# A branch product's operand pages in another order, its weight parts cut earlier, and the first down weights requested a unit ahead

## The chip, the core and the metric

The kernel runs on one core of one Trainium2 chip. Such a core has a matrix engine (TensorE, PE in the profile, with its weight loads as PEld), three engines for elementwise work (VectorE = DVE, ScalarE = ACT, GpSimd = POOL), a queue engine that only issues transfers (SyncE = SP) and 16 DMA engines that all transfers share. SBUF is the on-chip memory of 128 partitions; PSUM, in banks, takes what TensorE computes. Each engine takes its instructions in the order in which the program lists them. The metric is the time of one execution in device microseconds; lower is better.

## The reference

One layer of a streaming encoder on 1024 prompt rows and 32 sample rows (1056 columns in the kernel), float32. Cut to what surrounds the change:

```python
h = _rms_norm(x, g_pre_mix)
z = h @ w_in                       # q_A k_A v_A q_B f_B i_B og_B gate_A gate_B
ya = _sink_attention(...)          # branch A, 16 heads, window of 3 chunks
yb = _hgrn2(...)                   # branch B, gated linear recurrence
mix = jax.nn.sigmoid(ga) * (ya @ w_br_a) + jax.nn.sigmoid(gb) * (yb @ w_br_b)
x = x + _rms_norm(mix @ w_out, g_post_mix)
a, u = jnp.split(_rms_norm(x, g_pre_ffn) @ w_up, 2, axis=-1)
ac = b_conv + sum(ap[:, j:j + t] * w_conv[j] for j in range(3))
x = x + _rms_norm((jax.nn.gelu(ac) * u) @ w_down, g_post_ffn)
x = x + (pe @ w_ple) * jax.nn.sigmoid(x @ w_ple_gate)
```

## The kernel before

All products run at float32 precision on TensorE out of two parts: each operand is cut into a high part (a cast on ScalarE) and a low part (the operand less its high part, a subtraction on VectorE), and three matmuls (high x high, high x low, low x high) make one product. The large products are done in Strassen's manner: seven products of half-size blocks in place of eight, from sums of blocks that are made beforehand and kept in DRAM.

The program goes through these stages: the input product with attention and recurrence woven in; the last gate blocks (`stream(tail...)`, matmuls L205 to L207, results X, Y, Z evacuated by ScalarE into `gt` at L297 and stored to `tb_d`); the branch product `ya @ w_br_a` (`a_unit`, matmuls L1616 to L1620); `yb @ w_br_b`, the output product, the up product with 22 units (`up_unit`, L2297 to L2299), the down product (`d_unit`, L2418 to L2420) and the last gate.

**Operands of the branch product.** `opa[i, p]` is the operand of product i (0 to 6) for half p of the columns: a page `oa` of 128 x 2 x 4 x 264 floats. `a_load` (L1528) takes the page and asks for a transfer of 528 KB into its second half; `a_split` (L1537) casts the high part into the first half (L1534, ScalarE) and subtracts (L1535, VectorE). Pages have names such as r6 or l0; the r-pages lie in a pool `rp` on the right side of SBUF, where the tiles of the stages before lay. A page gets its address when its name is first asked for, in the order of asking; a transfer into it waits until the old tiles at that address have been read or stored for the last time. Before, the names were asked for as the loads were: r6, r1, r3, r5, r7 for the first five (issued on GpSimd), then r4, r0, r2 on SyncE.

**Weight parts.** `a_raw` (L1504) loads a pair of raw blocks `wa` (2 x 256 KB, two buffers, SyncE), `a_prepare(n)` (L1514) casts and subtracts the next block into `wt` (L1522, L1523), and asks for a further pair ahead. Eight buffers hold `wt`.

**What sets the order.** The dictionary `small` hangs work on the pieces of the last three gate blocks; `during` does the same for the steps of the branch product. `behind(S, V)` ties work to the last instruction of ScalarE and VectorE. Between these ties, a scheduling layer places every instruction in its engine's order, transfers too, so the order of the code isn't the order on an engine. In the branch product the bank of a first result is freed by a copy `as` (L1625, ScalarE).

**Down weights.** `d_raw` (L2050) loads a pair of raw blocks `wd`; before, the first call came out of `d_prepare` from step 4 of the last up unit on.

Of the kernel before, what the change touches and what calls it, by code (L numbers as in the profile page):

```python
# [17 lines left out]
P = 128  # L18
# [12 lines left out]
H = 264  # L31
# [28 lines left out]
def layer_kernel(  # L60
# [256 lines left out]
    with right("ap") as ap:  # L317
# [279 lines left out]
        def pinned(f, *engines):  # L597
            with behind(*engines):
                f()
# [333 lines left out]
        blocks, small = [(lambda w=w: w, 2, out) for w, out in zip(ws, outs)], {}  # L933
# [138 lines left out]
    small = {2 * n: [lambda n=n: pinned(lambda: b_prepare(n), V)] for n in range(3)}  # L1072
# [14 lines left out]
    with right("bp") as bp:  # L1087
# [309 lines left out]
        pieces, small = [], {}  # L1397
# [82 lines left out]
    def page(pool, n, shape, name):  # L1480

        s = f"{'r' if pool is rp else 'l'}{n}"
        s = home.get(s, s)
        return (rp if s[0] == "r" else lq).tile(shape, F32R, tag=f"pg{s[1:]}", name=nm(name))

    def page_at(s, shape, name):
        return page(rp if s[0] == "r" else lq, s[1:], shape, name)

    def columns8(s, name):
# [9 lines left out]
    at_a = {0: ("r6", "r5"), 1: ("r1", "r7"), 2: ("r3", "r4"), 3: ("r0", "r2"), 4: ("l0", "l1"),  # L1499
            5: ("l2", "l3"), 6: ("l4", "l5")}  # L1500
# [24 lines left out]

    opa = {}

    def a_load(i, p, queue=dma):  # L1528
        t = opa[i, p] = page_at(at_a[i][p], [P, 2, 4, H], "oa")
        src = sa_d[i][:, :, p] if i in sa_d else ya_v[:, min(i, 1), i // 6][:, :, p]  # L1530
        queue(t[:, 1].bitcast(F32), src)

# [7 lines left out]
    def both(f, *a):  # L1540
        with behind(S, V):
            f(*a)

    small = {}
    first_a = [(i, p) for p in range(2) for i in range(3)]
    for i, p in first_a[:5]:
        a_load(i, p, gdma)
    for m, (i, p) in enumerate(first_a[:5]):
        small[m + 1] = [lambda i=i, p=p: both(a_split, i, p)]
    for m in range(3):  # L1550
        small[m + 1].append(lambda m=m: both(a_prepare, m))
    for m, (i, p) in enumerate(((2, 1), (3, 0), (3, 1))):
        small[m + 3].append(lambda i=i, p=p: a_load(i, p))
    stream(tail[3:], small)
    lctx.close()
    pctx.close()
# [3 lines left out]
    with right("mp") as mp:  # L1560
# [91 lines left out]
        def during(s, f, *a):  # L1652
            steps_a.setdefault(s, []).append((f, a))
# [13 lines left out]
            both(load_next)  # L1667

        for n, (i, p) in enumerate((i, p) for i in (4, 5, 6) for p in range(2)):
            during(2 * n, a_load, i, p)  # L1670
            during(9 + n + n // 2, both, a_split, i, p)
        for n, (i, p) in enumerate(((2, 1), (3, 0), (3, 1))):
            during(2 * n + 1, both, a_split, i, p)
        for n in range(4):
# [375 lines left out]
    def d_raw():  # L2050

        k = len(raw_d)
        t = wp.tile([P, KT, P], F32, tag="wr", name=nm("wd"), bufs=2)
        raw_d.append(t)
        for a in range(2):
            pt, c, i = D_ORDER[2 * k + a]
            j0, n = KP[pt]
            z_ = slice(j0, j0 + n)
            src = w_d[i][:, c, z_] if i in w_d else dv[:, i // 2 % 2 + i // 5, i // 5, c, z_]
            dma(t[:, 4 * a:4 * a + n], src)  # L2060
# [52 lines left out]
    t = tr_bank()  # L2113
# [166 lines left out]
    def up_unit(u):  # L2280
        X, Y, Z = (pf.tile([P, 2, 512], F32, tag="st", name=nm("st"), bufs=3) for _ in range(3))
        ab = fp.tile([P, 4 + T], F32, tag="ab", name=nm("ab"), bufs=2)
        G.memset(ab[:, 0:2], 0.0)
        us = us0 if u == 0 else Up[:, u % 2, :].bitcast(F32)
        us4 = us.rearrange("p (a h c) -> p a h c", a=2, h=2)
        w = {}

        def mults(i, t, first, ps):
            n = 7 * u + i
            if i not in w:  # L2290
                w[i] = ready_w[n]
            for p in ps:
                for k in range(4):
                    wh, wl = w[i][:, 0, k, :], w[i][:, 1, k, :]
                    xh, xl = ops[p][i][:, 0, k, :], ops[p][i][:, 1, k, :]
                    o = t[:, p, 0:H]
                    E.matmul(o, wh, xh, start=first and k == 0, stop=False, skip_group_check=True)  # L2297
                    E.matmul(o, wh, xl, start=False, stop=False, skip_group_check=True)  # L2298
                    E.matmul(o, wl, xh, start=False, stop=k == 3, skip_group_check=True)  # L2299

        def v(t, ps):
            return t[:, ps[0]:ps[-1] + 1, 0:H]

        def after(i, ps):
            x, y, zz = v(X, ps), v(Y, ps), v(Z, ps)
            sl = slice(ps[0], ps[-1] + 1)
            if i == 0:
                S.copy(s1c[:, sl], x)  # L2308
            elif i == 1:
                V.tensor_tensor(U2[:, sl], s1c[:, sl], y, op=ALU.subtract)  # L2310
            elif i == 2:
                V.tensor_tensor(ab[:, 2:2 + T].rearrange("p (a h c) -> p a h c", a=2, h=2)[:, sl, 0, :],
                                x, rb4[:, sl, 0, :], op=ALU.mult)
            elif i == 3:
                V.tensor_tensor(nU3[:, sl], y, s1c[:, sl], op=ALU.subtract)
            elif i == 4:
                V.tensor_tensor(us4[:, sl, 1, :], nU3[:, sl], zz, op=ALU.subtract)
            elif i == 5:
                V.tensor_tensor(us4[:, sl, 0, :], y, s1c[:, sl], op=ALU.subtract)
            elif i == 7:  # L2320

                S.copy(t12[:, sl], zz)
            elif i == 8:
                V.tensor_tensor(nU3[:, sl], nU3[:, sl], t12[:, sl], op=ALU.add)
            else:
                V.tensor_tensor(t12[:, sl], U2[:, sl], zz, op=ALU.add)

        def done():

            V.tensor_tensor(ab[:, 2:2 + T].rearrange("p (a h c) -> p a h c", a=2, h=2)[:, :, 1, 0:232],  # L2330
                            t12[:, :, 0:232], rb4[:, :, 1, 0:232], op=ALU.mult)
            for p, o in ((0, 2 + 496), (1, 2 + 1026)):
                V.tensor_tensor(ab[:, o:o + 32], t12[:, p, 232:H], rb4[:, p, 1, 232:H], op=ALU.mult)
            tail_of.append(ff_tail(u, ab, us))
            next(tail_of[0])


        order = ((0, X, True, (0,)), (1, Y, True, (1,)), (2, X, False, (2,)), (3, Y, False, (3,)),
                 (4, Z, True, (4,)), (5, Y, False, (5,)), (6, Z, False, (6,)))
        first_ = order[:2] + ((2, X, False, ()),) + order[3:6] + ((6, Z, False, (2, 6)),)  # L2340
        early = ((0, X, True, (0,)), (6, Z, True, (7,)), (2, X, False, ()), (1, Y, True, (1,)),
                 (3, Y, False, (3, 8)), (4, Z, False, (4, 6)), (5, Y, False, (2, 5)))
        for ps, steps in (((0,), first_), ((1,), early)) if u == 0 else (((0, 1), order),):
            for n, (i, t, first, then) in enumerate(steps):
                if u:
                    prepare(7 * u + n + AHEAD)
                elif ps == (1,):
                    with behind(S, V):
                        prepare(n + AHEAD + 2)
                mults(i, t, first, ps)  # L2350
                if u == NF - 1:
                    if i < 3:
                        for p in range(2):
                            load_op(0, p, i)
                    if n in (3, 5, 6):
                        split_ops(0, {3: 0, 5: 1, 6: 2}[n])
                if ps == (1,) and n == 1:
                    with behind(E):
                        x1_t.append(pair_norm(1, 1.0 / D, late=True))
                if ps == (1,) and n == 4:  # L2360
                    with behind(E):
                        x1_t[0]()
                for a in then:
                    with behind(*((V,) if ps == (0,) and a == 2 else ())):
                        after(a, ps)
                if n == 1:
                    with behind(V):
                        tail_rest(u)
                if u == 1 and n == 3:
                    with behind(V):  # L2370
                        tail_rest(0)
                if u > 1 and n == 2 + u % 2:
                    if u % 2 == 0:
                        sums_of.append(act_sums(u // 2 - 1))
                    with behind(V):
                        next(sums_of[-1])
                if u == 0 and ps == (0,):
                    last_ops(n)
                if 2 <= u < 18 and n == 4:
                    w_sum((u - 2) // 2, 2 + u % 2)  # L2380
        done()
# [409 lines left out]
    t = tr_bank()  # L2791
# [26 lines left out]
    t = tr_bank()  # L2818
# [5 lines left out]
    t = tr_bank()  # L2824
# [40 lines left out]
```

## Time and profile before

| | |
|---|---|
| Time, median of 3 runs | 1954.24 us (1953.73 to 1957.8) |
| The profiled execution | 1954.29 us, its span 1952.5 us |
| TensorE busy | 1929.3 us |
| VectorE, ScalarE, GpSimd busy | 1452.2, 1012.4, 308.5 us |
| TensorE's longest wait | 5.0 us, at the first matmul of the branch product |
| DMA, mean | 155 GB/s, 302.19 MB |
| TensorE clock granted, mean | 0.998 of full |

The profile is of one execution. A view of waits names an engine and line, what it waited for, and microseconds in total, times, and the longest. In the timeline a row is: start, length, engine, line, operation, out<-in, shape, count, and in brackets the idle time ahead of it with what ended it. SPq is SyncE's queue of transfers; the time of such a row is that of the issue, not of the transfer.

### The profile page before, as it was taken

The page shows a single profiled execution, that of the slowest core. Times are in us where ns is not written, and L with a number is a line of the kernel's source. Part 1 is how long each engine was busy: PE and PEld are TensorE (multiplying, and loading weights), DVE is VectorE, ACT ScalarE, POOL GpSimd, SP SyncE. Part 2 cuts the span into 40 slices and gives each one's busy share as a digit, 9 for nine tenths or more (in the row PEclk, how much of TensorE's full clock was granted, in tenths as well). Part 3 has the DMA queues.
Part 4 walks back from the last instruction along what each step waited for, and adds up shares of the span by engine and source line. Part 5 has one row for each costly group of instructions (what it writes and reads, how often), then busy time and mean ns, then how long its engine had stood idle before and what let it go on. Part 6 is the DMA issues. An engine that isn't in the chain of part 4 may idle for free.

```text
span 1952.5 us, 38068 instructions
## 1 busy us (share of the span) xinstructions
PE 1929.3 (99%) x14619; PEld 1911.8 (98%) x14619; DVE 1452.2 (74%) x3160; ACT 1012.4 (52%) x2182; POOL 308.5 (16%) x419
## 2 busy tenths in 40 slices
PE   8999999999999999989999999999999999999998
PEld 8999999999999999989999999999999999999998
DVE  6777777788888888657655778778777786768872
ACT  7667777666656666543324763333333346534432
POOL 2111111010101110010001023343443410000000
PEclk9999999999999999999999999999999999999999
DMA  8534543433637563487749582434665357755343
GB/s 267 153 112 122 135 124 96 139 104 102 155 114 166 97 121 76 123 268 237 219 140 303 175 297 92 139 120 153 139 135 160 103 166 243 217 185 156 116 131 88
DMA packets 310507, 302.19 MB, mean 155 GB/s; under 512 B 14293, under 2 KB 276344, under 8 KB 310325
## 3 DMA queue, kind: packets, MB, share of 16 engines
q1 hardware_dynamic: 277269, 229.57, 37.8%
q0 software_dynamic: 32928, 70.14, 15.7%
q8 instruction: 115, 1.88, 0.4%
q14 instruction: 67, 0.55, 0.1%
q10 hardware_dynamic: 128, 0.06, 0.0%
HBM read 213.48 MB, written 115.16 MB: 168 GB/s over the span
## 4 chain that ended last, share of the span: by engine, by line
PE 86%; DVE 5%; DMA 3%; ACT 3%; issue 2%; POOL 0%; SPq 0%; ACTq 0%; DVEq 0%; POOLq 0%
PE st L2299 7%; PE st L2298 7%; PE st L2297 7%; PE mm L205 6%; PE mm L206 6%; PE mm L207 6%; PE st L2418 4%; PE st L2420 4%; PE st L2419 4%; PE Y L1119 2%; PE G L1122 2%; PE st L205 2%; PE G L1121 2%; PE Y L1122 2%; PE Y L1121 2%; PE G L1119 2%
## 5 line engine op out<-in xcount | busy, mean ns | idle before, releaser
L2297 PE MATMUL st<-op,wt 128*128 128x264 f32 x1232 | 348.9, 283 | 2.3 <-ACT Sp L2308 1.4
L2299 PE MATMUL st<-op,wt 128*128 128x264 f32 x1232 | 349.7, 284 | 0.0
L2298 PE MATMUL st<-op,wt 128*128 128x264 f32 x1232 | 347.6, 282 | 0.0
L2297 PEld LDWEIGHTS st<-op,wt 128*128 128x128 f32 x1232 | 231.2, 188 | 4.0 <-ACT Sp L2308 2.0
L2298 PEld LDWEIGHTS st<-op,wt 128*128 128x128 f32 x1232 | 231.4, 188 | 0.0
L2299 PEld LDWEIGHTS st<-op,wt 128*128 128x128 f32 x1232 | 230.8, 187 | 0.0
L2418 PE MATMUL st<-dop,wt 128*128 128x264 f32 x616 | 174.4, 283 | 1.2 <-ACT S L2433 1.2
L2420 PE MATMUL st<-dop,wt 128*128 128x264 f32 x616 | 174.3, 283 | 0.0
L2419 PE MATMUL st<-dop,wt 128*128 128x264 f32 x616 | 173.9, 282 | 0.0
L1965 ACT CAST wt<-wu 128x512 fp32r<-128x512 f32 x126 | 75.9, 618 | 178.1 <-POOL wu L1974 71.6
L205 PE MATMUL mm<-La,wh 128*128 128x384 f32 (+1 forms) x480 | 158.2, 330 | 0.0
L206 PE MATMUL mm<-Lb,wh 128*128 128x384 f32 (+1 forms) x480 | 155.3, 324 | 0.6 <-DVE Lb L781 0.6
L207 PE MATMUL mm<-La,wl 128*128 128x384 f32 (+1 forms) x480 | 154.9, 323 | 0.1
L1966 DVE TENSOR_TENSOR wt<-wu,wt 128x512 fp32r<-128x512 f32 x126 | 86.5, 695 | 46.7 <-ACT wt L1965 46.7
L2418 PEld LDWEIGHTS st<-dop,wt 128*128 128x128 f32 x616 | 115.6, 188 | 1.7 <-ACT S L2433 1.4
L2419 PEld LDWEIGHTS st<-dop,wt 128*128 128x128 f32 x616 | 115.7, 188 | 0.0
L2420 PEld LDWEIGHTS st<-dop,wt 128*128 128x128 f32 x616 | 115.4, 188 | 0.0
L2071 ACT CAST wt<-wd 128x512 fp32r<-128x512 f32 (+1 forms) x84 | 49.1, 586 | 90.6 <-PE st L2420 77.9
L206 PEld LDWEIGHTS mm<-Lb,wh 128*128 128x128 f32 x480 | 90.4, 189 | 1.7 <-DVE Lb L781 1.5
L207 PEld LDWEIGHTS mm<-La,wl 128*128 128x128 f32 x480 | 90.2, 188 | 0.5 <-DVE wl L756 0.5
L1119 PE MATMUL G<-La,wt 128*128 128x288 f32 x288 | 90.4, 314 | 0.0
L205 PEld LDWEIGHTS mm<-La,wh 128*128 128x128 f32 x480 | 90.2, 188 | 0.2
(602 smaller groups left out, 6249.9 us busy)
## 6 DMA issues: line engine op xcount, KB each, us to landing
wu<-in_w_up_dram SPq DMA_DIRECT2D x42, 512.0 KB
wu<-in_w_in_dram SPq DMA_DIRECT2D x36, 512.0 KB
w_d<-in_w_down_dram POOLq DMA_DIRECT2D x24, 704.0 KB, 6.8
a_d<-Up SPq DMA_DIRECT2D x22, 528.0 KB
wr<-in_w_in_dram SPq DMA_DIRECT2D x21, 512.0 KB
s_d<-sm SPq DMA_DIRECT2D x40, 264.0 KB
dop<-s_d SPq DMA_DIRECT2D x16, 528.0 KB
wr<-in_w_out_dram SPq DMA_DIRECT2D x16, 512.0 KB
```

Source lines behind the costliest of these rows:

```text
L205: E.matmul(ps, wh, a, start=first and n == 0, stop=False)
L206: E.matmul(ps, wh, b, start=False, stop=False)
L207: E.matmul(ps, wl, a, start=False, stop=last and n == len(ks) - 1)
L1119: E.matmul(o, wh, x[0][k], start=first and k == 0, stop=False, skip_group_check=True)
L1121: E.matmul(o, wh, x[1][k], start=False, stop=False, skip_group_check=True)
L1966: V.tensor_tensor(t[:, 1], src, t[:, 0].bitcast(F32), op=ALU.subtract)
L2297: E.matmul(o, wh, xh, start=first and k == 0, stop=False, skip_group_check=True)
L2298: E.matmul(o, wh, xl, start=False, stop=False, skip_group_check=True)
L2299: E.matmul(o, wl, xh, start=False, stop=k == 3, skip_group_check=True)
L2418: E.matmul(o, wh, xh_, start=first and k == 0, stop=False, skip_group_check=True)
L2419: E.matmul(o, wh, xl_, start=False, stop=False, skip_group_check=True)
L2420: E.matmul(o, wl, xh_, start=False, stop=k == ng - 1, skip_group_check=True)
```

## The change

`a_load` no longer takes the page; a new `a_page` does. The pages of the first three products and of product 3 are taken ahead of any load, in the order (3,0), (3,1), (2,1), (1,1), (0,1), (2,0), (1,0), (0,0), so that r0, r2, r4, r7, r5, r3, r1, r6 lie in this order in the pool. The weight parts are tied to pieces 0, 0, 2, 3, 4, 5 of the gate blocks, six in all, where three were tied to pieces 1, 2, 3. The two loads for product 3 are asked for in steps 0 and 1 of the branch product. In the last up unit, two calls of `d_raw` come at step 0.

```diff
+    def a_page(i, p):
+        opa[i, p] = page_at(at_a[i][p], [P, 2, 4, H], "oa")
+
     def a_load(i, p, queue=dma):
-        t = opa[i, p] = page_at(at_a[i][p], [P, 2, 4, H], "oa")
+        t = opa[i, p]
...
+    for i, p in [(3, 0), (3, 1), *first_a[::-1]]:
+        a_page(i, p)
     for i, p in first_a[:5]:
         a_load(i, p, gdma)
     for m, (i, p) in enumerate(first_a[:5]):
         small[m + 1] = [lambda i=i, p=p: both(a_split, i, p)]
-    for m in range(3):
-        small[m + 1].append(lambda m=m: both(a_prepare, m))
-    for m, (i, p) in enumerate(((2, 1), (3, 0), (3, 1))):
-        small[m + 3].append(lambda i=i, p=p: a_load(i, p))
+    for n, m in enumerate((0, 0, 2, 3, 4, 5)):
+        small.setdefault(m, []).append(lambda n=n: both(a_prepare, n))
+    small[3].append(lambda: a_load(2, 1))
...
         for n, (i, p) in enumerate((i, p) for i in (4, 5, 6) for p in range(2)):
+            a_page(i, p)
             during(2 * n, a_load, i, p)
             during(9 + n + n // 2, both, a_split, i, p)
+        for p in range(2):
+            during(p, a_load, 3, p)
...
                 if u == NF - 1:
+                    if n == 0:
+                        d_raw()
+                        d_raw()
                     if i < 3:
```

**GpSimd, at the end of the recurrence.** A row is line, operation, out<-in and shape; the numbers in names are buffers. In brackets are the semaphores on which the instruction waits (HW for transfers of SyncE, SW for those of GpSimd). S is the last state's load, the rows behind it the loads of the first five pages. Before:

```order
L1325 DMA S_10736<-in_state_hgrn_dram 128x128 [waits DMASW1_49,DVE_49,PE_49]
L1531 DMA oa_10847<-ya_d 128x4x264 [waits DMAHW3_49,DMAHW2_49,DMAHW4_49,DMAHW1_49,DMAHW5_49,DMAHW0_49,DMAHW6_49,DVE_49,DMAHW7_49,Activation_49,Pool_49]
L1531 DMA oa_10849<-sa_d_108 128x4x264 [waits DMAHW5_49,DMAHW1_49,DMAHW7_49,DMASW3_49,PE_49]
L1531 DMA oa_10851<-ya_d 128x4x264 [waits PE_49,Activation_49]
L1531 DMA oa_10853<-ya_d 128x4x264 [waits DMASW7_49]
L1531 DMA oa_10855<-sa_d_108 128x4x264 [waits DMASW0_49]
```

And now:

```order
L1325 DMA S_10736<-in_state_hgrn_dram 128x128 [waits DMASW1_49,DVE_49,PE_49]
L1534 DMA oa_10854<-ya_d 128x4x264 [waits DMAHW5_49]
L1534 DMA oa_10853<-sa_d_108 128x4x264 [waits DMAHW4_49]
L1534 DMA oa_10852<-ya_d 128x4x264 [waits DMAHW3_49]
L1534 DMA oa_10851<-ya_d 128x4x264 [waits DMASW7_49]
L1534 DMA oa_10850<-sa_d_108 128x4x264 [waits DMAHW2_49,DMASW0_49]
```

The order is the same, the waits are others. Before, the first page waited among others for the last stores `yb_d<-sg`; now the HW counts that the loads wait for are those of the loads of the four tiles TL, and the SW counts those of earlier sums of weight blocks. The pages (3,0) and (3,1) have taken over the place of the tiles `sg` and `S`.

**ScalarE, through the last gate blocks.** The rows from the evacuation of block G to that of block Z. Before:

```order
L297 ACTIVATE gt_10833<-G_10808 128x384
L297 ACTIVATE gt_10882<-X_10857 128x288
L1534 CAST oa_10847<-oa_10847 128x1056
L1522 CAST wt_10893<-wa_10887 128x512
L297 ACTIVATE gt_10926<-Y_10896 128x384
L1534 CAST oa_10849<-oa_10849 128x1056
L1522 CAST wt_10911<-wa_10887 128x512
L1534 CAST oa_10851<-oa_10851 128x1056
L1522 CAST wt_10934<-wa_10890 128x512
L1522 CAST wt_11003<-wa_10890 128x512
L1534 CAST oa_10853<-oa_10853 128x1056
L297 ACTIVATE gt_10968<-Z_10939 128x384
```

And now, behind the same evacuation of G:

```order
L1522 CAST wt_10879<-wa_10873 128x512
L1522 CAST wt_10882<-wa_10873 128x512
L297 ACTIVATE gt_10897<-X_10860 128x288
L1537 CAST oa_10854<-oa_10854 128x1056
L297 ACTIVATE gt_10935<-Y_10902 128x384
L1537 CAST oa_10853<-oa_10853 128x1056
L1522 CAST wt_10920<-wa_10876 128x512
L1537 CAST oa_10852<-oa_10852 128x1056
L1522 CAST wt_10940<-wa_10876 128x512
L1537 CAST oa_10851<-oa_10851 128x1056
L1522 CAST wt_10962<-wa_10917 128x512
L297 ACTIVATE gt_10977<-Z_10944 128x384
```

Two `wt` casts moved ahead of the evacuation of X, and five in place of four stand ahead of that of Z; the four `oa` casts kept their places.

**ScalarE, at the start of the branch product.** The rows from there to the copy that frees the first bank. Before:

```order
L297 ACTIVATE gt_10968<-Z_10939 128x384
L1534 CAST oa_10855<-oa_10855 128x1056
L1522 CAST wt_11009<-wa_10931 128x512
L1522 CAST wt_11012<-wa_10931 128x512
L1625 COPY as_11027<-st_11001 128x264
```

And now:

```order
L297 ACTIVATE gt_10977<-Z_10944 128x384
L1537 CAST oa_10850<-oa_10850 128x1056
L1522 CAST wt_10982<-wa_10917 128x512
L1522 CAST wt_11038<-wa_10959 128x512
L1537 CAST oa_10849<-oa_10849 128x1056
L1629 COPY as_11031<-st_11017 128x264
```

One more `oa` cast stands ahead of the copy, and the second `wt` cast reads a raw pair (`wa_10959`) whose loads on SyncE wait for VectorE's half of the fourth part (`wt_10940`). On TensorE, eight matmuls of the second column's first product now stand ahead of the first column's third, which waits for that copy. On SyncE the pair `wa_10917` is asked for ahead of the loads of (2,1), (3,0) and (3,1), where it stood behind them; the `wd` and `dop` loads at the end of the up product stand in the same rows, with the same waits, as before.

## The prediction

> **What bounds the kernel now.** The page comes first, then TensorE's waits, then the timeline around the longest wait.
>
> ```profile
> span 1952.5 us, 38068 instructions
> PE 1929.3 (99%) x14619; PEld 1911.8 (98%) x14619; DVE 1452.2 (74%) x3160; ACT 1012.4 (52%) x2182; POOL 308.5 (16%) x419
> ...
> PE st L1616 <- ACT gt L297: 5.0, 1, 5.0
> ...
> PE st L2418 <- ACT S L2433: 1.2, 1, 1.2
> ```
>
> TensorE is busy for 99% of the span and idle for 1952.5 - 1929.3 = 23.2 us. No other engine comes near, so only idle TensorE time, or time at a reduced clock, can be won. The largest single wait, 5.0 us, stands at the first matmul of the branch product (L1616), and it is what the first two edits are about. The third edit sits ahead of the down product, whose first wait is 1.2 us.
>
> The timeline of TensorE at the start of the branch product (start, length, engine, line, operands, and in brackets the idle time before with what ended it), with two stretches of the table of windows:
>
> ```profile
> 849.06 0.34 PE L207 MATMUL Z<-La,wl 128*128 128x384 f32 x1
> 854.37 0.59 PE L1616 MATMUL st<-oa,wt 128*128 128x264 f32 x1 [4.97 <-ACT gt L297]
> ...
> 859.22 0.39 PE L1616 MATMUL st<-oa,wt 128*128 128x264 f32 x1 [0.31 <-ACT as L1625]
> 859.45 0.28 PE L1618 MATMUL st<-oa,wt 128*128 128x264 f32 x1
> ...
> 860.29 0.28 PE L1620 MATMUL st<-oa,wt 128*128 128x264 f32 x1
> 860.41 0.28 PE L1616 MATMUL st<-oa,wt 128*128 128x264 f32 x1
> 855.00:858.00 3.00, 3.00 (x17) 3.00 (x17) 2.08 (x3) 1.38 (x2) 0.00 (x0) 0.60 0.91 257
> 862.00:880.00 18.00, 18.00 (x151) 18.00 (x150) 11.95 (x18) 10.96 (x16) 1.91 (x4) 1.00 0.98 311
> ```
>
> (The windows give length, busy time of PE, PEld, DVE, ACT, POOL with counts, granted clock, DMA share, GB/s; where one number is missing the order is the same. In the first of the two the granted clock is 0.60, in the second 1.00.) Three losses stand here: the 4.97 us, the low clock behind it, and 0.31 us before the 25th matmul. The 33rd and 34th matmul of the product start at 860.29 and 860.41, 0.12 us apart at full clock; I measure the gain at the 34th, since from 862 on TensorE is busy without a gap.
>
> Why the first matmul waits shows on ScalarE (ACT) and GpSimd (POOL):
>
> ```profile
> 823.76 0.59 POOL L1325 DMA_DIRECT2D S<-in_state_hgrn_dram  x1 [16.59 <-PE so L1370]
> 841.10 0.78 POOL L1531 DMA_DIRECT2D oa<-ya_d  x1 [16.75 <-DMA yb_d<-sg]
> 841.15 0.41 ACT L297 ACTIVATE gt<-X 128x288 f32<-128x288 f32 x1 [3.08 <-PE X L207]
> 846.00 1.07 ACT L1534 CAST oa<-oa 128x1056 fp32r<-128x1056 f32 x1 [4.43 <-DMA oa<-ya_d]
> 846.98 0.61 ACT L1522 CAST wt<-wa 128x512 fp32r<-128x512 f32 x1
> 847.50 0.48 ACT L297 ACTIVATE gt<-Y 128x384 f32<-128x384 f32 x1
> 847.91 1.08 ACT L1534 CAST oa<-oa 128x1056 fp32r<-128x1056 f32 x1
> ...
> 852.85 1.07 ACT L1534 CAST oa<-oa 128x1056 fp32r<-128x1056 f32 x1 [0.63 <-DMA oa<-ya_d]
> 853.83 0.48 ACT L297 ACTIVATE gt<-Z 128x384 f32<-128x384 f32 x1
> ...
> 858.27 0.62 ACT L1522 CAST wt<-wa 128x512 fp32r<-128x512 f32 x1 [0.21 <-DMA wa<-in_w_br_a_dram]
> 858.80 0.37 ACT L1625 COPY as<-st 128x264 f32<-128x264 f32 x1
> ```
>
> TensorE needs the PSUM bank that the last gate block Z used, and gt<-Z frees it. ScalarE takes its work in order, and four casts of operand pages (oa) stand ahead of gt<-Z; each waits for a transfer that GpSimd could only issue at 841.10, when the last store out of the old tile on that page (yb_d<-sg) had landed. So the wait is one for late transfers, passed on by a queue.
>
> **The change part by part.** *Page order.* The five first pages now lie where the tiles TL lay; what their transfers wait for are those tiles' loads, issued long before:
>
> ```profile
> 348.11 2.09 SPq L988 DMA_DIRECT2D TL<-t_d  x4
> 800.00:838.00 38.00, 38.00 (x262) 37.89 (x261) 18.34 (x63) 16.38 (x53) 0.99 (x3) 1.00 0.32 102
> 846.00:848.00 2.00, 2.00 (x13) 2.00 (x12) 0.90 (x1) 2.00 (x4) 0.00 (x0) 1.00 1.06 379
> ```
>
> Ahead of them on GpSimd stands only the load of S at 823.76, so they can be issued from 824.35, 16.75 us earlier, at 0.78 us each: until 828.3. They bring 5 x 528 KB = 2.70 MB; the 102 GB/s that already flow from 825 to 838 are another 1.3 MB; at 379 GB/s both take 10.6 us, until about 836. All five have landed before gate block X ends at 841.15, and the 4.43 us and 0.63 us that ScalarE waits for pages go. The matmuls of the last gate blocks hide these transfers; what they cost if that cover fails is rival 3. GpSimd itself is idle there.
>
> *Weight parts.* Two casts wt now stand ahead of gt<-X, at 838.0; their lower halves are free on VectorE. ScalarE then has gt<-X, one oa, gt<-Y, then three oa and three wt, then gt<-Z. Y's last matmul is the row 844.90 below and ends at 845.23, so gt<-Y starts at 845.26. With the spacing of the rows above (oa to the next 0.98, wt 0.52, gt 0.41) gt<-Z starts at 845.26 + 0.41 + 3 x 0.98 + 3 x 0.52 = 850.17, and the first matmul 0.54 later (853.83 to 854.37): **850.7** in place of 854.37. TensorE then idles 4.97 - 3.66 = 1.3 us. The clock behind such a gap is shown at the down product:
>
> ```profile
> 844.90 0.33 PE L207 MATMUL Y<-La,wl 128*128 128x384 f32 x1
> 1621.32 0.39 PE L2418 MATMUL st<-dop,wt 128*128 128x264 f32 x1 [1.23 <-ACT S L2433]
> 1611.00:1622.00 11.00, 9.77 (x81) 9.56 (x80) 9.23 (x18) 6.46 (x10) 0.00 (x0) 1.00 1.02 308
> ```
>
> After 1.23 us the clock stayed at 1.00 and the next matmuls came every 0.12 us, so I take full clock. The program now has 32 matmuls (8 of another column among them) before it needs the copy as; the 33rd could start at 850.7 + 0.23 + 31 x 0.12 = 854.7.
>
> *What is late next.* The copy as, which frees the first bank, now stands behind one oa, two wt, and one more oa. The second wt reads a raw weight tile whose buffer comes free only when VectorE has made the fourth part's lower half, and SyncE asks for it then:
>
> ```profile
> 849.02 1.26 DVE L1535 TENSOR_TENSOR oa<-oa 128x1056 fp32r<-128x1056 f32 x1
> 850.20 0.68 DVE L1523 TENSOR_TENSOR wt<-wa,wt 128x512 fp32r<-128x512 f32 x1
> 810.78 0.94 SPq L1512 DMA_DIRECT2D wa<-in_w_br_a_dram  x2
> 850.91 0.52 SPq L1512 DMA_DIRECT2D wa<-wa_d  x1
> 857.43 0.62 ACT L1522 CAST wt<-wa 128x512 fp32r<-128x512 f32 x1 [1.62 <-DMA wa<-wa_d]
> 812.00:814.00 2.00, 2.00 (x18) 2.00 (x17) 0.55 (x1) 0.98 (x4) 0.00 (x0) 1.00 0.83 249
> S<-in_state_hgrn_dram POOLq DMA_DIRECT2D x1, 64.0 KB, 2.1
> ```
>
> ScalarE ends the third page's cast at 845.67 + 0.98 + 0.52 + 1.07 = 848.24; VectorE, still at a weight half, begins that page's lower half near 848.5, and 1.18 later (849.02 to 850.20) the fourth part's, which takes 0.68: the transfer is issued at **850.5**, on a SyncE queue that holds only stores ahead of it. Its duration is the unknown term. Before, the same kind took 857.43 - 850.91 = 6.5 us, with the engines saturated (window at 846: share 1.06); that is the upper end. The lower end is that it costs ScalarE no wait. Now 2.70 MB have moved forward, and the 2.5 MB asked for from 840 to 846 (one raw pair of 512 KB, three pages, stores of 144 and 192 KB) are through near 848 at 379 GB/s, so the light case is nearer: the pair issued at 810.78 moved its 512 KB almost wholly at 249 GB/s within 812 to 814. I take 2.1 us of the 64 KB row plus 192 KB at 249 GB/s = **2.9 us**: landed at 853.4. Then wt 0.52, oa 0.98, and the matmul 0.42 after as starts (858.80 to 859.22): 855.3 for the 33rd, 855.5 for the 34th, a new wait of 0.6 us. Against 860.41 the gain is **4.9 us**. With no wait for the weight it is 860.41 - 854.85 = 5.6, with 6.5 us it is 1.3.
>
> The Trainium skill prices it otherwise: in "DMA: Bandwidth & Descriptors", section "Anatomy of one DMA — SWDGE (gpsimd) path", a transfer takes about 2.0 us plus its bytes at 436 GB/s. That would be 2.6 us as an estimate, and a gain of 5.2; the 6.5 us row shows that it doesn't hold when the engines are saturated.
>
> *First down weights.* In SyncE's order the first two wd pairs and the dop loads stand exactly where they stood, with the same waits; only buffer numbers differ. The change costs and brings 0 here, and the wait of 1.23 us stays; if it did go, that would be 1.2 us more.
>
> *Later on.* From 862 TensorE runs without a gap; transfers and casts ahead of it are now no later than before in relation to it, so I let the whole gain reach the end. The sum: 1954.29 us of the profiled execution (0.05 above the median of 1954.24) - 4.9 = **1949.4 us**.
>
> **Rivals.** (1) *The new wait takes most of it back*: the late weight transfer takes 3.6 to 6.5 us because it still meets other traffic. For it speaks the old 6.5 us, against it the 2.70 MB moved out of the way. Gain 4.2 down to 1.3, at 6.5 us 1953.0.
>
> (2) *The pages don't come earlier.* Something holds GpSimd's issues to about 841 after all. Then the additional wt ahead of gt<-Z costs 0.52 and the 0.31 wait is saved: 1954.5. Against it: GpSimd's row at 841.10 names the store as its only late releaser.
>
> (3) *Slower: the early pages collide with the operands of the gate blocks.* SyncE asks for four Lb pieces of 192 KB in the same microseconds:
>
> ```profile
> 825.91 1.42 SPq L1437 DMA_DIRECT2D Lb<-h_d  x3
> 841.08 0.33 PE L206 MATMUL Y<-Lb,wh 128*128 128x384 f32 x1
> 842.00:844.00 2.00, 2.00 (x13) 2.00 (x12) 0.00 (x0) 0.00 (x0) 2.00 (x3) 1.00 0.71 153
> ```
>
> TensorE reads them at 841.08. Pages and Lb are 3.5 MB; at 379 GB/s they end 9 us after 825.9. But while GpSimd issued its pages before, from 842 to 844, only 153 GB/s flowed. A wait of TensorE on Lb would first use up all the old losses together (from 849.4 on without a gap the 34th matmul would start at 849.4 + 0.1 + 33 x 0.12 = 853.5, against 860.41: 6.9 us), so it decides once Lb lands after 848; at 153 GB/s all through that is 848.7. At 130 GB/s Lb ends at 852.7, and the time is 1954.29 + 11.6 - 6.9 = 1959. Against it: the slow rate held for 2 us while issuing went on, and 379 GB/s followed by 846; and the stretch from 800 to 838 left two thirds of the DMA engines' time free.
>
> **How the numbers follow.** The forecast, gain 4.3 to 5.6, has 0.66; rival 1 0.19; rival 2 0.09; rival 3 0.06. The range takes the first two, with both ends of the unknown transfer and half a microsecond for the spread of runs: 1948.2 to 1953.5. A measurement of this kernel tells about 0.2% (3.9 us) from no change. Faster by more: the forecast, 0.66, and a little of rival 1's near end: 0.68. Within: the rest of rival 1, rival 2: 0.26. Slower: 0.06.
>
> **What would show it.** Right: GpSimd's five page issues at 824 to 829; ScalarE's oa casts with no wait for a transfer; the wait of st L1616 on gt near 1.3 us with the clock at 1.00 behind it; a wait on as under 1 us; st L2418 still waiting 1.2 us. Wrong: issues at 841, a wt cast held past 854.5 by wa, a wait of TensorE on Lb, or a low clock after the short gap (then 0.7 us less, since the wait on as covers part of it).

## The result, and the profile after

The changed kernel takes 1950.12 us (median of 15 runs, 1948.9 to 1953.69), the kernel before 1954.63 us beside it (15 runs, 1953.73 to 1958.28). The ratio is 0.9978, with a 95% interval of 0.997 to 0.9986: faster by about 4.3 us by the ratio, 4.5 us by the medians. The forecast was 1949.4 us.

The busy times from the changed kernel's profile, and three rows of its table of waits (line numbers have moved: L1620 is the branch product, was L1616; L2428 the down product, was L2418):

```profile
span 1948.2 us, 38057 instructions
...
PE 1927.2 (99%) x14619; PEld 1910.0 (98%) x14619; DVE 1453.3 (75%) x3160; ACT 1012.4 (52%) x2182; POOL 307.3 (16%) x419
```

```profile
PE st L1620 <- ACT as L1629: 1.6, 2, 1.4
...
PE st L2428 <- ACT S L2443: 1.4, 1, 1.4
PE st L1620 <- ACT gt L297: 1.3, 1, 1.3
```

The wait of 5.0 us on gt is down to 1.3 us. A new wait on the copy as has come in (1.4 us, the longer of two), and the wait of the down product is still there. The timeline of GpSimd and of ScalarE in the changed kernel shows why the first one went:

```profile
822.82 0.59 POOL L1325 DMA_DIRECT2D S<-in_state_hgrn_dram  x1 [16.59 <-PE so L1370]
823.39 0.79 POOL L1534 DMA_DIRECT2D oa<-ya_d  x1
```

```profile
844.37 0.49 ACT L297 ACTIVATE gt<-Y 128x384 f32<-128x384 f32 x1 [2.79 <-PE Y L207]
...
849.23 0.49 ACT L297 ACTIVATE gt<-Z 128x384 f32<-128x384 f32 x1
...
853.35 0.62 ACT L1522 CAST wt<-wa 128x512 fp32r<-128x512 f32 x1 [2.15 <-DMA wa<-in_w_br_a_dram]
853.88 1.07 ACT L1537 CAST oa<-oa 128x1056 fp32r<-128x1056 f32 x1
854.85 0.37 ACT L1629 COPY as<-st 128x264 f32<-128x264 f32 x1
```

GpSimd asks for its first page at 823.39 instead of 841.10, and between gt<-Y and gt<-Z ScalarE waits for nothing. Behind gt<-Z it waits 2.15 us for a raw weight pair, and the copy as stands behind that cast. TensorE in the same stretch, and SyncE's ask for that pair:

```profile
848.11 0.34 PE L207 MATMUL Z<-La,wl 128*128 128x384 f32 x1
849.77 0.39 PE L1620 MATMUL st<-oa,wt 128*128 128x264 f32 x1 [1.32 <-ACT gt L297]
...
855.27 0.39 PE L1620 MATMUL st<-oa,wt 128*128 128x264 f32 x1 [1.35 <-ACT as L1629]
855.50 0.29 PE L1622 MATMUL st<-oa,wt 128*128 128x264 f32 x1
```

```profile
843.03 1.28 SPq L1534 DMA_DIRECT2D oa<-sa_d  x2
...
849.51 0.39 SPq L1512 DMA_DIRECT2D wa<-in_w_br_a_dram  x1
```

The pair took 853.35 - 849.51 = 3.84 us from ask to cast; 2.9 us had been assumed. The row at 855.50 is the product's 34th matmul, at which the prediction measures the gain. The two profiles do not reach the branch product at the same time (Z's last matmul starts at 849.06 before and at 848.11 here), so I count from there: 860.41 - 849.06 = 11.35 us before, 855.50 - 848.11 = 7.39 us after. The gain at the 34th matmul is 3.96 us, of the 4.9 predicted. Two stretches of the table of windows (the columns as in the prediction):

```profile
830.00:838.00 8.00, 8.00 (x57) 7.96 (x56) 3.44 (x15) 2.06 (x7) 0.00 (x0) 1.00 0.99 351
...
848.00:850.00 2.00, 0.68 (x5) 0.36 (x4) 2.00 (x3) 2.00 (x4) 0.00 (x0) 1.00 1.00 351
```

The pages fill the DMA engines from 830 to 838 (102 GB/s there before), with TensorE busy throughout. In the microseconds ahead of the ask for the pair, from 848 to 850, they are full again (351 GB/s, where 92 GB/s flowed from 840 to 842). The clock is 1.00 in both.

### The profile page after: what moved, and what is told of

It is laid out like the page before. It is cut to its first block, busy times and chain, and to the rows that moved or that the text cites. A ratio compares the mean times of both kernels' runs of the same rounds, so it can differ in the third digit from the quotient of the medians.

```text
span 1948.2 us, 38057 instructions
## 1 busy us (share of the span) xinstructions
PE 1927.2 (99%) x14619; PEld 1910.0 (98%) x14619; DVE 1453.3 (75%) x3160; ACT 1012.4 (52%) x2182; POOL 307.3 (16%) x419
## 5 line engine op out<-in xcount | busy, mean ns | idle before, releaser
L2428 PE MATMUL st<-dop,wt 128*128 128x264 f32 x616 | 174.4, 283 | 1.4 <-ACT S L2443 1.4
L2428 PEld LDWEIGHTS st<-dop,wt 128*128 128x128 f32 x616 | 115.6, 188 | 1.9 <-ACT S L2443 1.6
```

Of the source, the lines that this page charges most:

```text
L2428: E.matmul(o, wh, xh_, start=first and k == 0, stop=False, skip_group_check=True)
```

## The experiments

Two numbers are read from each profile, both from the start of Z's last matmul, which takes out the differences of some 2 us with which the profiles reach it: the time to the product's 34th matmul, and the time to the end of the span. "pair" is the time from SyncE's ask for the raw pair that ScalarE waits for ahead of the copy as, to the cast that reads it first (it is the fourth pair and the seventh part; the expectations, counting otherwise, call it the pair of the third weight part, and the cast that of the sixth). A 0 stands where the profile shows no wait; an empty field means that the number isn't used. The ratio is that of the timed runs to the kernel before, run on the same chip.

| kernel | Z's last | 34th | between | gain there | wait on gt | wait on first as | pair | Z's last to end | ratio, 95% interval |
|---|---|---|---|---|---|---|---|---|---|
| before | 849.06 | 860.41 | 11.35 | | 4.97 | 0.31 | | 1103.4 | |
| whole change | 848.11 | 855.50 | 7.39 | 3.96 | 1.32 | 1.35 | 3.84 | 1100.1 | 0.9978, 0.997 to 0.9986 |
| again (e8) | 847.84 | 855.61 | 7.77 | 3.58 | 1.32 | 1.73 | 4.22 | 1101.9 | 0.9983, 0.9974 to 0.9992 |
| a third time (e11) | 848.92 | 856.11 | 7.19 | 4.16 | 1.32 | 1.17 | 3.64 | 1099.5 | 0.9977, 0.9968 to 0.9986 |
| without down edit (e3) | 848.80 | 855.16 | 6.36 | 4.99 | 1.32 | 0.34 | 2.81 | 1098.2 | 0.9979, 0.997 to 0.9988 |
| pages only (e1) | 849.29 | 855.05 | 5.76 | 5.59 | 1.32 | 0 | | 1099.1 | 0.9969, 0.9959 to 0.9979 |
| pages only again (e9) | 847.72 | 853.47 | 5.75 | 5.60 | 1.32 | 0 | | 1099.1 | 0.9975, 0.9966 to 0.9984 |
| weight parts only (e2) | 848.26 | 862.22 | 13.96 | -2.61 | 8.11 | 0 | | 1106.8 | 1.0008, 0.9999 to 1.0017 |
| copy first (e4) | 849.32 | 855.08 | 5.76 | 5.59 | 1.32 | 0 | 3.58 | 1097.8 | 0.9977, 0.9968 to 0.9985 |
| late pages (e5) | 848.45 | 854.87 | 6.42 | 4.93 | 1.32 | 0.37 | 2.86 | 1102.0 | 0.9998, 0.9989 to 1.0007 |
| filled (e6) | 849.88 | 854.96 | 5.08 | 6.27 | 0.63 | 0 | 4.81 | 1097.5 | 0.9971, 0.996 to 0.9983 |
| filled again (e10) | 848.32 | 853.40 | 5.08 | 6.27 | 0.63 | 0 | 4.47 | 1099.9 | 0.9967, 0.9955 to 0.9979 |
| filled, down (e7) | 849.55 | 854.63 | 5.08 | 6.27 | 0.63 | 0 | 3.54 | 1097.7 | 0.9974, 0.9964 to 0.9983 |

The intervals of the timed ratios are about 0.2% (4 us) wide, so they hardly tell these kernels apart; the waits in the profiles do.

**Pages only (e1, and again e9).** The order of the pages as in the change; everything else as before. The edit is against the whole change:

```diff
-    for n, m in enumerate((0, 0, 2, 3, 4, 5)):
-        small.setdefault(m, []).append(lambda n=n: both(a_prepare, n))
-    small[3].append(lambda: a_load(2, 1))
+    for m in range(3):
+        small[m + 1].append(lambda m=m: both(a_prepare, m))
+    for m, (i, p) in enumerate(((2, 1), (3, 0), (3, 1))):
+        small[m + 3].append(lambda i=i, p=p: a_load(i, p))
...
-        for p in range(2):
-            during(p, a_load, 3, p)
...
-                    if n == 0:
-                        d_raw()
-                        d_raw()
```

> Only the order of the pages is changed; weight parts, third-page loads and down weights as before. Theory A (the early page transfers are the whole gain, and the weight edit only moves a cast ahead of the copy as): the page issues on GpSimd start near 823, gt Z frees its bank near 850.7 and TensorE's wait on gt is 1.3 us, as with the whole change; the raw pair of the third weight part is asked for 1.2 to 2 us earlier, so the wait on as is 0 to 0.3 us instead of 1.35, and the span is 5.0 to 5.6 us below before's 1952.5: 1946.9 to 1947.5, about 1 us below the whole change (ratio 0.9971 to 0.9975). Theory B (the weight parts begun earlier are needed as well): without them the product runs out of weight parts, a wait on wt or as of over 1.35 us shows, and the span is above 1948.2, up to before's 1952.5.

> The page order alone, beside the whole change on one chip. From Z's last matmul to the end of the span before took 1103.4 us; the page order alone took 1099.1 in its first profile, the whole change 1100.1, 1101.9 and (without the down edit) 1098.2. Theory A (the weight edit costs the wait on the first copy, 0.3 to 1.7 us, and sometimes the clock): no wait on the first copy as here, the 34th matmul 5.76 us behind Z's last again, the clock at 1.00, and the timed median below that of the whole change. Rival (the later copies give it back, 0.53 us in the first profile): the same median within 0.5 us.

TensorE and ScalarE of the first of these profiles:

```profile
849.29 0.34 PE L207 MATMUL Z<-La,wl 128*128 128x384 f32 x1
850.95 0.39 PE L1621 MATMUL st<-oa,wt 128*128 128x264 f32 x1 [1.32 <-ACT gt L297]
...
867.99 0.39 PE L1621 MATMUL st<-oa,wt 128*128 128x264 f32 x1 [0.53 <-ACT as L1630]
```

```profile
852.84 0.62 ACT L1522 CAST wt<-wa 128x512 fp32r<-128x512 f32 x1 [0.21 <-DMA wa<-in_w_br_a_dram]
853.37 0.37 ACT L1630 COPY as<-st 128x264 f32<-128x264 f32 x1
```

The wait on gt is the same 1.32 us: the page order alone removes the long wait. The first copy as comes in time, and the gain at the 34th matmul is 5.6 us in both profiles, more than the whole change has in any of its four. So at this place the weight edit, with the loads that were moved along with it, costs 0.6 to 2.0 us. At a later copy the pages-only kernel gives 0.53 us back (0.62 in e9), and to the end it gains 4.3 us both times. The span of 1948.4 us in e1 missed the 1946.9 to 1947.5 expected; 1946.8 in e9. Timed, its medians were 1949.01 and 1949.61, against 1949.91 (e3) and 1950.08 (e11) for the whole change's order on the same chips: in the expected direction, but within the intervals, and the second difference, 0.47 us, is inside the half microsecond that the rival allowed. That the pages alone are the faster kernel is shown at the 34th matmul, not in the timed runs.

**Weight parts only (e2).** The other half: the kernel before, with the parts tied to earlier places (the loads of (2,1) and of product 3 stay where they were). The edit is against the kernel before:

```diff
-    for m in range(3):
-        small[m + 1].append(lambda m=m: both(a_prepare, m))
+    for n, m in enumerate((0, 0, 2, 3, 4, 5)):
+        small.setdefault(m, []).append(lambda n=n: both(a_prepare, n))
```

> Only the weight parts are begun earlier; pages, their loads and the down weights as before. Theory A: GpSimd's page issues still wait for the store out of the old tile until 841, ScalarE's oa casts still wait for transfers, and the wait of about 5 us on gt stays, with the low clock behind it: span 1952.0 to 1953.0 (ratio 0.9997 to 1.0003). Theory B (the weight parts carry a share of the gain by themselves): the wait on gt falls by 1 us or more, span below 1951.5.

Neither happened: it loses 2.61 us at the 34th matmul and 3.4 us to the end. TensorE, then SyncE and GpSimd, then the DMA issues from 838 to 858 (528 KB each, with the median us from issue to landing), in this kernel:

```profile
856.70 0.59 PE L1616 MATMUL st<-oa,wt 128*128 128x264 f32 x1 [8.11 <-ACT gt L297]
```

```profile
839.14 0.56 SPq L1512 DMA_DIRECT2D wa<-wa_d  x1
839.75 0.61 SPq L1512 DMA_DIRECT2D wa<-in_w_br_a_dram  x1
...
840.25 0.78 POOL L1531 DMA_DIRECT2D oa<-ya_d  x1 [16.69 <-DMA yb_d<-sg]
```

```profile
oa<-ya_d POOLq DMA_DIRECT2D x3, 528.0 KB, 11.0
oa<-sa_d POOLq DMA_DIRECT2D x2, 528.0 KB, 11.6
```

and the same view of the kernel before:

```profile
oa<-ya_d POOLq DMA_DIRECT2D x3, 528.0 KB, 7.5
oa<-sa_d POOLq DMA_DIRECT2D x2, 528.0 KB, 8.2
```

Two casts done early free a raw buffer early, so a raw pair of 512 KB is asked for at 839.14, in front of the pages, where before the next one came at 850.91. The pages, still late on GpSimd, then take 11 us in place of 7.5, and gt<-Z waits for them longer. At 379 GB/s the pair accounts for 1.38 us of that; what makes up the rest stays open. In the whole change the same early ask (840.53) does these pages no harm, since they have landed by then.

**Without the down edit (e3)**, and the changed kernel again (e8, e11). In e3 only the two calls of d_raw are left out:

```diff
-                    if n == 0:
-                        d_raw()
-                        d_raw()
```

> The whole change without the two raw down weights asked for a unit ahead. Theory A (that edit moves nothing): span 1948.2 within 0.3 us, TensorE's first wait of the down product on S 1.2 to 1.4 us as with the change and before it. Theory B (the early ask does hide or cause something at the down product): that wait differs by 0.5 us or more, and the span with it.

> The changed kernel itself once more, beside the others on their chip. Both theories: wait on gt 1.3 us. The raw pair of the third weight part took 3.84 us in its first profile and 2.81 us in the run without the down edit, with the same order of instructions there; a third sample should lie between 2.7 and 4.0 us, and the wait on as moves with it one to one (0.3 us at 2.8, 1.35 us at 3.84).

> The changed kernel a third time. Wait on gt 1.3 us. The wait on the first copy moves with the time of the raw pair from ask to cast: 0.35 us at 2.8, 1.35 at 3.84, 1.73 at 4.22. If that wait is 1.7 us or more the clock falls to 0.5 behind it for some 3 us, as in the second profile; below 1.4 us it stays at 1.00.

The order of the instructions is that of the whole change, so these are four samples of one stretch. The down product's wait on S was 1.0 us in e3, and 1.4, 1.1 and 1.4 us with the edit (1.2 us before the change): no effect to be seen beyond that spread. The span of e3, 1947.0 us, missed the 1948.2 within 0.3 that theory A expected; what differs in e3 is the first copy. SyncE, ScalarE and TensorE of e3, and then ScalarE, TensorE and the windows of e8:

```profile
850.20 0.39 SPq L1512 DMA_DIRECT2D wa<-in_w_br_a_dram  x1
...
853.01 0.62 ACT L1522 CAST wt<-wa 128x512 fp32r<-128x512 f32 x1 [1.12 <-DMA wa<-in_w_br_a_dram]
...
854.94 0.39 PE L1620 MATMUL st<-oa,wt 128*128 128x264 f32 x1 [0.34 <-ACT as L1629]
```

```profile
853.47 0.62 ACT L1522 CAST wt<-wa 128x512 fp32r<-128x512 f32 x1 [2.54 <-DMA wa<-in_w_br_a_dram]
...
855.39 0.39 PE L1620 MATMUL st<-oa,wt 128*128 128x264 f32 x1 [1.73 <-ACT as L1629]
```

```profile
854.00:855.00 1.00, 0.00 (x0) 0.00 (x0) 0.69 (x1) 1.00 (x3) 0.00 (x0) 1.00 0.98 294
855.00:856.00 1.00, 0.61 (x4) 0.62 (x5) 0.64 (x2) 0.85 (x3) 0.00 (x0) 0.87 0.81 237
856.00:857.00 1.00, 1.00 (x6) 1.00 (x6) 1.00 (x2) 0.00 (x0) 0.00 (x0) 0.50 0.85 240
...
859.00:860.00 1.00, 1.00 (x10) 1.00 (x9) 0.00 (x0) 0.95 (x2) 0.45 (x1) 0.93 1.02 299
```

The pair took 2.81, 3.64, 3.84 and 4.22 us, and the wait on as was 0.34, 1.17, 1.35 and 1.73 us: pair less 2.47 to 2.49 us each time. One moves with the other, one to one, as the expectations said; the 4.22 us of e8 lie outside the 2.7 to 4.0 us expected. In e8 the clock fell to 0.50 behind that wait, from about 855.7 (0.87 in its window) to 859.1 (0.93): 3.4 us at half speed, or 1.7 us lost, which the 34th matmul does not yet show; its gain to the end is only 1103.4 - 1101.9 = 1.5 us. In e11, with a wait of 1.17 us, the clock stayed at 1.00, as expected below 1.4 us; a wait of 1.7 us or more at this place did not come again, so that half of the expectation rests on e8 alone.

**Copy first (e4).** The whole change, with the cast that waits for the pair held behind the first copy:

```diff
-                    a_prepare(n_a[0] + 5)
+                    with behind(*((S,) if n_a[0] == 1 else ())):
+                        a_prepare(n_a[0] + 5)
```

> The whole change, and the cast of the sixth weight part held behind the first copy as on ScalarE, so that as is no longer behind a cast that waits for its raw weights. Theory A (the 1.35 us wait on as is the late weight transfer passed on by ScalarE's order): the wait on as goes to 0 to 0.2 us, the cast still waits for its pair, behind as; the 34th matmul comes 1.35 us earlier relative to Z's last, and the span is 1946.6 to 1947.2 (ratio 0.9971 to 0.9974). Theory C (the weight is needed by TensorE itself just as late): the wait reappears within the product's next 100 matmuls on wt or on the next copy, and the span stays within 0.4 us of 1948.2.

ScalarE in this kernel:

```profile
852.73 0.38 ACT L1630 COPY as<-st 128x264 f32<-128x264 f32 x1 [0.32 <-PE st L1625]
854.30 0.62 ACT L1522 CAST wt<-wa 128x512 fp32r<-128x512 f32 x1 [1.19 <-DMA wa<-in_w_br_a_dram]
```

The pair is as late as ever (3.58 us), but the copy no longer stands behind it. TensorE runs on, the 34th matmul gains 5.59 us, and the span of 1947.1 is within the forecast; no wait took the place of the one removed. So the weight is not needed by TensorE that early: the wait was ScalarE's order alone. The timed median (1950.06, ratio 0.9977) does not show this gain, where 0.9971 to 0.9974 was expected; 1.4 us lies within its interval.

**Late pages (e5).** The whole change, with the two pages of operand 3 asked for behind the pair instead of ahead of it:

```diff
+        def late(f, *a):
+            with behind(nc.sync):
+                f(*a)
...
-            during(p, a_load, 3, p)
+            during(p, late, a_load, 3, p)
```

> The whole change, with the two pages of operand 3 asked for behind the raw pair of the third weight part instead of ahead of it: 1056 KB less stand in front of that pair. Theory A (the pair takes 2.8 to 3.8 us because the tail of that traffic is still flowing when it is asked for): from the ask to the start of the cast it takes at most 2.5 us, the DMA rate between 846 and 850 falls below 250 GB/s, and the wait on the first copy as is 0 to 0.3 us. Theory C (the 3 us are the pair's own, whatever else flows): 2.8 us or more from the ask to the cast, and the wait on as stays at 0.3 to 1.4 us. Both: the operand-3 pages now land near 859, so a cast of theirs may hold the third copy as; a wait there of up to 1 us says nothing on the question.

A window, SyncE and ScalarE of this kernel, and TensorE's third copy wait:

```profile
848.00:850.00 2.00, 0.79 (x5) 0.47 (x3) 2.00 (x4) 2.00 (x5) 0.00 (x0) 1.00 0.09 31
```

```profile
849.86 0.38 SPq L1512 DMA_DIRECT2D wa<-in_w_br_a_dram  x1
...
852.72 0.62 ACT L1522 CAST wt<-wa 128x512 fp32r<-128x512 f32 x1 [1.17 <-DMA wa<-in_w_br_a_dram]
...
862.50 1.07 ACT L1537 CAST oa<-oa 128x1056 fp32r<-128x1056 f32 x1 [5.23 <-DMA oa<-sa_d]
...
864.42 0.39 PE L1620 MATMUL st<-oa,wt 128*128 128x264 f32 x1 [1.27 <-ACT as L1629]
```

The engines were nearly empty when the pair was asked for (31 GB/s), and it still took 2.86 us. Theory A had said at most 2.5 us: that part falls. So 2.86 us is the pair's time with hardly any other traffic, in this one profile, and the order of ScalarE costs 0.37 us on as even then. The other 0.8 to 1.4 us, which three of the four samples with the pages in front show, were absent here. They fit the tail of other traffic that still flows when the pair is asked for. In the first microsecond after the ask no traffic flowed in e5 and 130 GB/s in e3 (2.86 and 2.81 us); 181 GB/s in the first profile of the change, 211 in e11 and 305 in e8 went with 3.84, 3.64 and 4.22 us. In the filled kernels below it was 237 GB/s with 3.54 us (e7), 369 with 4.47 (e10) and 375 with 4.81 (e6). It is no strict rule: in e4 333 GB/s went with 3.58 us. So this cause is likely and not shown. The late pages themselves hold the third copy and cost 1.27 us there, later waits on VectorE of 0.5 and 0.4 us come in as well, and the kernel is no faster than before (0.9998): a transfer put off for another's sake is late itself.

**Filled (e6, again e10).** The whole change and the pin of e4, with two page casts and one weight cast (the expectation says one of each) moved into ScalarE's idle time ahead of gt<-Y; a list keeps the gates' evacuations behind the casts there:

```diff
-    for m, (i, p) in enumerate(first_a[:5]):
-        small[m + 1] = [lambda i=i, p=p: both(a_split, i, p)]
-    for n, m in enumerate((0, 0, 2, 3, 4, 5)):
+    for (i, p), m in zip(first_a[:5], (1, 2, 2, 3, 5)):
+        small.setdefault(m, []).append(lambda i=i, p=p: both(a_split, i, p))
+    for n, m in enumerate((0, 0, 2, 3, 3, 5)):
```

> The whole change, the copy held ahead of the cast as in the run of that name, and in addition one page cast and one weight cast moved from between the gates of Y and Z into ScalarE's idle time before the gate of Y; only one page cast and two weight casts stand between the two gates. Theory A (the remaining 1.3 us wait on gt is ScalarE's queue, 0.8 us, and a fixed 0.54 us from the gate to the matmul): the wait on gt is 0.5 to 0.7 us, the 34th matmul comes 6.2 to 6.4 us earlier than before relative to Z's last, against 5.6 with the copy alone; span 1946.0 to 1946.8. Rival: the weight pairs asked for later on SyncE (behind two stores) hold the next copy, and a wait of 0.5 us or more on as or wt takes the gain back: span 1947 or more.

> The filled kernel once more. Theory A: wait on gt 0.6 us and none on the first copy, Z's last to the end 1097.5 us within 0.7, the lowest median of the three kernels on this chip, 1 to 3 us under the whole change. Rival (waits further on take its gain back): the same median as the page order alone, within 0.5 us, or above it.

TensorE and ScalarE of e6:

```profile
850.85 0.39 PE L1626 MATMUL st<-oa,wt 128*128 128x264 f32 x1 [0.63 <-ACT gt L300]
```

```profile
850.31 0.49 ACT L300 ACTIVATE gt<-Z 128x384 f32<-128x384 f32 x1 [1.67 <-PE Z L207]
```

ScalarE now waits for TensorE at gt<-Z, not the other way round; what is left of the wait (0.63 us) is the way from Z's end over gt to the matmul. The gain at the 34th matmul is 6.27 us in both profiles, as forecast. The spans (1947.4, 1948.2) are above the 1946.0 to 1946.8 expected, and e10's 1099.9 us to the end misses its 1097.5 within 0.7: in e10 the wait of the down product on S was 2.1 us, against 1.1 in e6, and behind it the clock fell to 0.50 for some 3.4 us (1.7 us lost), which it did not do in e6 (the last section has the rows). Its medians, 1948.8 and 1948.43, are the lowest beside the whole change on the same chips (1950.75 and 1950.08): 1.95 and 1.65 us lower, though the intervals overlap. It beats the kernel before clear of the interval, and the change in this stretch by both profiles; to the end of the span e10's 1099.9 us are no better than the 1099.5 us of e11.

**Filled, and the down product's copies (e7).** The same pattern in the down product: copies that free banks stand behind weight casts. I held the casts behind the copies, and the copies in the order in which their banks fill:

```diff
-                d_prepare(n_d[0] + D_AHEAD)
+                with behind(*((S,) if n_d[0] in (3, 4) else ())):
+                    d_prepare(n_d[0] + D_AHEAD)
...
-            S.copy(o, x)
+            with behind(*((S,) if (c, i) in ((0, 1), (0, 2), (1, 0)) else ())):
+                S.copy(o, x)
```

> As the filled kernel, and in the first units of the down product the copies that free the PSUM banks are held ahead of the casts of later weights, in the order in which their banks fill; TensorE then has the next bank's matmuls ahead of those that need the newest copy. Theory A (the 0.8 to 1.4 us wait on S is the same pattern, a copy behind casts that wait for transfers): that wait goes below 0.3 us, and the span is 0.6 to 1.3 us below the filled kernel's in the down stage. Rival: the raw down weights, asked for later, hold the next parts, and a wait on wt or on a later copy of 0.5 us or more takes its place.

TensorE and ScalarE there:

```profile
1616.40 0.39 PE L2434 MATMUL st<-dop,wt 128*128 128x264 f32 x1 [2.18 <-ACT T L2450]
```

```profile
1615.75 0.60 ACT L2450 COPY T<-st 128x528 f32<-128x528 f32 x1 [1.52 <-DVE Up L2212]
```

The wait on S is gone, and one of 2.18 us on T stands in its place. It is not the rival that I had named, a late weight: by its row the copy waits for an instruction of VectorE, the last on Up (L2212), most likely because T lies where that instruction still reads. In e6, in the older order, TensorE has no wait on T. No gain.

## Why the prediction was right, and where it was not

- **The pages come earlier: right.** Issued from 823.39 (824.35 predicted, in a trace that runs 0.95 us earlier), landed before they are read, no wait of an oa cast for a transfer up to gt<-Z. They took the DMA engines until 838 and not 836: the 102 GB/s in the sum is the mean from 800 to 838, and from 825 to 838 the kernel before moved 149 GB/s. TensorE never waited for Lb (rival 3); rival 2 is excluded by the same rows. That this edit alone brings the gain is shown by e1 and e9; e2 and e3 show that neither of the others does.
- **First matmul at 850.7, a wait of 1.3 us, full clock: right.** It came 1.66 us after the start of Z's last matmul (849.77 - 848.11); the forecast was 1.64. The wait was 1.32 us in every kernel with the early pages and the old place of gt<-Z. e6 shows what it is made of: ScalarE's queue (0.69 us of it) and a way of 0.63 us that stays.
- **The new wait on as: the right mechanism, too small a size.** The term that failed is the raw pair's 2.9 us. It measured 2.81, 3.64, 3.84 and 4.22 us; the wait, which was to stay under 1 us, followed it one to one to 1.17, 1.35 and 1.73 us in three of four profiles, and e4 took it away by order alone. At 2.81 us the gain was 4.99 (4.9 predicted for 2.9), so the rest of the sum holds. What was wrong in the working of 2.9 is not the pair's time with little traffic, which e5 and e3 put at 2.8 to 2.9, but most likely the step that had the traffic of 840 to 846 "through near 848". It went by 379 GB/s from the start; from 840 to 842 only 92 GB/s flowed, so at 848 to 850 there were still 351 GB/s. That alone doesn't decide, since e3 moved 379 GB/s in the same stretch; e3 had the least traffic left once the pair was asked for. The estimate of 2.6 us by the Trainium skill ("DMA: Bandwidth & Descriptors", "Anatomy of one DMA — SWDGE (gpsimd) path") lies below all of them, even with the engines at 31 GB/s. That section is on transfers that GpSimd issues, though, and SyncE issues this pair; and the times here run to the start of the cast, not to the landing.
- **Rival 1 was priced too low.** Its condition, a transfer of 3.6 us or more, was met in three of the four profiles of this order. It had a chance of 0.19. The three lie at its near end, so the time hardly moved. The median came out 0.7 us above the forecast, but 0.4 us of that is the kernel before, 1954.63 us beside it where the sum began from 1954.24; the gain is 4.3 to 4.5 us of the 4.9. With an interval of 2.7 to 5.9 us on that gain, so close a hit is partly luck, and the timed runs can't tell the forecast from rival 1's near end; the profiles do.
- **A cost that was left out.** The clock was considered for the first gap alone. A second gap 4 us after it can bring the low clock after all (e8): 1.7 us more.
- **Down weights: right.** No effect in e3 against the others; the wait on S stays, between 1.0 and 1.4 us.
- **The gain reaches the end: right within what profiles tell.** 3.96 us at the 34th matmul against 3.3 us to the end, 4.16 against 3.9, 4.99 against 5.2 in the change's own order, the exception being e8 with its clock (3.58 against 1.5). In the other kernels it held less well: 5.59 and 5.60 against 4.3 in e1 and e9, 4.93 against 1.4 in e5, 6.27 against 3.5 in e10.
- **The parts were not priced one by one.** The sum took both edits together and so didn't show that the weight edit takes some of the page edit's gain back (0.6 to 2.0 us at the 34th matmul), nor that alone it loses (2.61 us there, e2).

## What to carry to other kernels

Where TensorE waits for an accumulator bank, look at what stands ahead of the evacuation on the evacuating engine: a cast that waits for a transfer passes its wait on to TensorE, and holding the copy ahead of the cast removes that without making the transfer any earlier. When a transfer is moved forward, follow what is asked for in the microseconds behind it, and take for the next transfer's duration the range of several executions: here 2.8 to 4.2 us in one and the same order of instructions. Starting work earlier can also bring a prefetch forward, in front of transfers that are needed sooner.

## What the runs showed of the hardware that was not expected

The TensorE clock does not follow the length of one gap. In e8 it fell to 0.50 behind a gap of 1.73 us, which came 4.2 us after another of 1.32 us; in the first profile of the change 1.35 us at that place left it at 1.00, and in e7 a gap of 2.18 us by itself did too, as this stretch of its windows shows:

```profile
1614.00:1616.00 2.00, 0.23 (x2) 0.02 (x1) 1.73 (x3) 0.48 (x2) 0.00 (x0) 1.00 0.69 245
1616.00:1618.00 2.00, 1.60 (x13) 1.60 (x14) 1.41 (x4) 2.00 (x5) 0.00 (x0) 1.00 0.78 309
```

In e10 a gap of 2.13 us, at the start of the down product as well and with no other gap near it, was followed by the low clock:

```profile
1615.51 0.39 PE L2434 MATMUL st<-dop,wt 128*128 128x264 f32 x1 [2.13 <-ACT S L2449]
1616.00:1617.00 1.00, 1.00 (x9) 1.00 (x8) 1.00 (x4) 0.80 (x3) 0.00 (x0) 0.69 0.21 77
1617.00:1618.00 1.00, 1.00 (x6) 1.00 (x6) 1.00 (x2) 0.92 (x3) 0.00 (x0) 0.50 0.85 338
```

The Trainium skill ("TensorE: Matmul & The Clock Gate", "HAM oscillation — how this bites in real kernels") gives the rule that gaps are to be avoided above about 3.4 us. By that rule no gap of the changed kernel would cost clock; e8 shows one of 1.73 us that did, and e10, in the filled kernel, one of 2.13 us. What decides between these and the 2.18 us of e7 was not tried, so it stays open; the low stretch lasted about 3.4 us in e8 and in e10.
